# A Strassen-style up projection: one weight-block sum formed by an accumulating DMA instead of by VectorE

## The chip, the core and the metric

The kernel runs on one core of one Trainium2 chip. The metric is the device time of one launch in microseconds. Inside the core, TensorE (PE) multiplies matrices, VectorE (DVE) and ScalarE (ACT) work on elements, GpSimd (POOL) and SyncE (SP) here mostly issue transfers between the chip's main memory and the on-chip memory. Each engine runs its own list of instructions strictly in order. An instruction that waits for a semaphore holds up everything behind it on its engine. L124 means line 124 of the kernel before.

## The reference

A decoder trunk of two layers on 528 positions (512 tokens and 16 learned ones) of width 1024, in float32. The part that the change touches is the first matrix product of the MLP:

```
for l in range(DEPTH):
    a = rmsnorm(h, mix_pre_g[l])
    ...
    h = h + rmsnorm(y @ w_out[l], mix_post_g[l])
    a = rmsnorm(h, mlp_pre_g[l])
    f = jnp.square(jax.nn.relu(a @ w_up[l])) @ w_down[l]
    h = h + rmsnorm(f, mlp_post_g[l])
```

`w_up` is 1024 x 4096 and `w_down` 4096 x 1024 in each layer.

## The kernel before

**Matrix products.** Each float32 operand is split in a rounded part `hi` and the rest `lo`. A product is three matmuls, hi·hi, hi·lo and lo·hi (`mm3`, L193 to L195). A weight tile is loaded by SP into a raw buffer `wraw` (five buffers of 256 KB, taken in turn), then `cast` makes `hi` on ACT (L108) and `lo = raw - hi` on DVE (L109). Casts run ahead of PE: a tile is prepared as soon as PE has released an old one (`tile_done`, `refill`).

**The MLP.** It goes in four chunks of 1024 hidden columns per layer. A chunk is eight "up" tiles (`a @ w_up`, relu, square) and eight "down" tiles that add into `z`. In chunk 0 the up tiles are plain. In chunks 1 to 3 two up tiles at a time, a pair, are computed by Winograd's form of Strassen's method: seven products of half depth instead of eight. There are four pairs in a chunk, three such chunks in a layer, two layers, so six such chunks and 24 pairs. In what follows p0 to p3 are the four pairs of one chunk.

**Weights of a pair.** `prep_pair` prepares them in seven steps n = 0 to 6. At n = 0 SP loads four blocks A11, A21, A22, A12 of 512 x 128 (L119). Four sums are then formed on DVE, each one instruction on 128 x 512 elements: S1 = A21 + A22 (L124), S2 = A11 - S1 (L125), S3 = A21 - A11 (L128, in place of A21) and S4 = A12 + S2 (L131, in place of S2). The steps cast A11, S2, S3, S1, A12, A22, S4 in this order. S1 and S2 live in the pool `u`, which has two buffers, so the S1 of a pair has the buffer of the S1 of the pair before. That buffer is free once step n = 3 of the pair before has cast it.

**Products of a pair.** `fast_pair` does seven products of 12 matmuls each in four banks of the accumulation memory: into b1 with B11, into b6 with T2, into b7 with T3, into b5 with T1, then on top of what is there into b1 with B21, into b7 with T4, into b5 with B22. DVE empties the banks in between (L955): u2 = p1 + b6, u3 = u2 + b7, then u3 + b5. The product with T4 writes onto b7, so PE must wait until DVE has read b7 for u3. The product with B22 writes onto b5, so it must wait until DVE has read b5 for u3 + b5.

**The order of the work.** The program is written tile by tile. A scheduler then fixes each engine's order at build time, from its own estimate of when things will be ready. So an edit in `prep_pair` can move instructions everywhere in the lists, and DVE's list mixes casts and sums for the next two pairs with the emptying of banks for the pair that PE is working on.

Of the kernel before, what the change touches and what calls it, by code (L numbers as in the profile page):

```python
# [11 lines left out]
ALU = mybir.AluOpType  # L12

P = 128
# [22 lines left out]
def trunk_kernel(ctx, tc, xT, gains, sinkb, sinkm, rope, masks, maskm, ident_in, w_in, w_out, w_up, w_down, outT):  # L37
    nc = tc.nc
    ACT, DVE, POOL, PE = nc.scalar, nc.vector, nc.gpsimd, nc.tensor
# [64 lines left out]
    def half():  # L104
        return wp.tile([P, 4, P], F32, tag="wraw", name="wraw", bufs=5)

    def cast(raw, hi, lo):
        ACT.activation(hi, raw, AF.Copy)  # L108
        DVE.tensor_tensor(lo, raw, hi.bitcast(F32), ALU.subtract)  # L109


    pair = {}

    def prep_pair(l, m, n):

        if n == 0:
            for name, k, mm in (("A11", 0, m), ("A21", 0, m + 1), ("A22", 4, m + 1), ("A12", 4, m)):
                pair[name] = half()
                nc.sync.dma_start(pair[name], w_up[l].rearrange("(k p) m -> p k m", p=P)[:, k:k + 4, P * mm:P * mm + P])  # L119
        flat = lambda t: t.rearrange("p k m -> p (k m)")  # L120
        f = wp.tile([P, KT, P], F32R, tag="w", name="wf", bufs=2 * CAP)
        if n == 1:
            pair["S1"], pair["S2"] = (utile()[:, :512].rearrange("p (k m) -> p k m", k=4) for _ in range(2))
            DVE.tensor_tensor(pair["S1"], pair["A21"], pair["A22"], ALU.add)  # L124
            DVE.tensor_tensor(pair["S2"], pair["A11"], pair["S1"], ALU.subtract)  # L125
        if n == 2:
            pair["S3"] = pair["A21"]
            DVE.tensor_tensor(pair["S3"], pair["A21"], pair["A11"], ALU.subtract)  # L128
        if n == 6:
            pair["S4"] = pair["S2"]  # L130
            DVE.tensor_tensor(pair["S4"], pair["A12"], pair["S2"], ALU.add)  # L131
        cast(pair[("A11", "S2", "S3", "S1", "A12", "A22", "S4")[n]], f[:, 0:4, :], f[:, 4:8, :])
        prepared.append((f[:, 0:4, :], f[:, 4:8, :]))

    def prep(beside=None):
# [5 lines left out]
        if kind == "upx":  # L141
            return prep_pair(l, *sub)
# [105 lines left out]
    def utile():  # L248
        return tp.tile([P, L + 2], F32, tag="u", name="u", bufs=2)
# [855 lines left out]
```

## Time and profile before

| what | value |
|---|---|
| time before, median of 2 runs | 1141.0 us (1140.63 and 1141.37) |
| the profiled execution, device time | 1140.6 us |
| its span from first to last instruction | 1138.8 us |
| mean granted TensorE clock over the span | 0.975 |
| DMA, all queues, mean over the span | 102.04 MB, 90 GB/s |
| DMA queue of SP (q1) | 100.15 MB, 30.4% of 16 engines' time |
| DMA queue of POOL (q0) | 0.21 MB, 0.1% |

The profiled execution lies 1.8 us above its span, and 0.4 us below the median. Durations in the trace include pipeline fill: two instructions of one engine overlap in part, so the distance between starts is shorter than the duration of one.

### The profile page before, as it was taken

To read this page: it belongs to the slowest core of one execution; us is meant where nothing else is said; L and a number is where in the kernel's file an instruction comes from. 1 tells how busy PE (TensorE), PEld (TensorE's weight loads), DVE (VectorE), ACT (ScalarE), POOL (GpSimd) and SP (SyncE) were. 2 spreads that over 40 slices of the span, in tenths; PEclk is the share of its full clock that TensorE was granted. 3 is DMA by queue.
4 is the path that set the end of the run, shared out by engine and by line. 5 is a ranking of instruction groups with operands and counts; after the bars stand their busy time and mean duration, and the time that the engine had idled before them with its cause. 6 is when DMAs were issued, how large, how long until landed. Compare 5 with 4: busy or idle time off the path is not lost.

```text
span 1138.8 us, 21453 instructions
## 1 busy us (share of the span) xinstructions
PE 1088.9 (96%) x8066; PEld 1042.9 (92%) x8066; DVE 822.3 (72%) x1941; ACT 641.2 (56%) x1542; POOL 20.2 (2%) x56
## 2 busy tenths in 40 slices
PE   8999889899999999999989997898999999999995
PEld 8999789899999999999978997898888988988995
DVE  7987867868486586586689878678855856856836
ACT  8665766655383274275456556666734734724732
POOL 3000000000000000000000000000000000000001
PEclk9999989899999999999989999898999999999998
DMA  9242122242243243144132421222422522522502
GB/s 263 66 124 65 38 75 68 81 117 70 66 131 102 61 126 112 50 119 130 43 88 59 116 63 47 66 75 75 123 81 65 148 85 65 156 77 67 147 1 75
DMA packets 197672, 102.04 MB, mean 90 GB/s; under 512 B 7424, under 2 KB 197520, under 8 KB 197568
## 3 DMA queue, kind: packets, MB, share of 16 engines
q1 hardware_dynamic: 196960, 100.15, 30.4%
q8 instruction: 63, 1.03, 0.4%
q14 instruction: 41, 0.34, 0.1%
q10 hardware_dynamic: 432, 0.32, 0.1%
q0 software_dynamic: 176, 0.21, 0.1%
HBM read 97.88 MB, written 2.10 MB: 88 GB/s over the span
## 4 chain that ended last, share of the span: by engine, by line
PE 87%; DVE 7%; ACT 3%; issue 1%; DMA 1%; SPq 0%; DVEq 0%; POOL 0%; ACTq 0%
PE ps L195 28%; PE ps L193 28%; PE ps L194 27%; PE ps L199 2%; DVE wlo L109 1%; PE ps L232 1%; ACT S L647 1%; DMA h<-in_xT 1%; DVE acc L277 1%; PE ps L693 1%; DVE p L281 1%; DVE a_lo L335 0%; DVE S L658 0%; DVE z L706 0%; DVE h L324 0%
## 5 line engine op out<-in xcount | busy, mean ns | idle before, releaser
L194 PE MATMUL ps<-f_lo,whi 128*128 128x256 f32 (+2 forms) x1072 | 326.1, 305 | 0.0
L195 PE MATMUL ps<-f_hi,wlo 128*128 128x256 f32 (+2 forms) x1072 | 325.4, 305 | 0.0
L193 PE MATMUL ps<-f_hi,whi 128*128 128x256 f32 (+2 forms) x1072 | 323.7, 306 | 0.0
L193 PE MATMUL ps<-a_hi,whi 128*128 128x256 f32 (+3 forms) x808 | 242.5, 302 | 7.2 <-ACT a_hi L330 6.2
L194 PE MATMUL ps<-a_lo,whi 128*128 128x256 f32 (+3 forms) x808 | 238.5, 295 | 4.6 <-DVE a_lo L335 4.1
L195 PE MATMUL ps<-a_hi,wlo 128*128 128x256 f32 (+3 forms) x808 | 237.1, 294 | 0.3 <-DVE wlo L109 0.3
L194 PEld LDWEIGHTS ps<-f_lo,whi 128*128 128x128 f32 x1072 | 201.7, 188 | 9.6
L195 PEld LDWEIGHTS ps<-f_hi,wlo 128*128 128x128 f32 x1072 | 201.9, 189 | 9.2
L193 PEld LDWEIGHTS ps<-f_hi,whi 128*128 128x128 f32 x1072 | 200.1, 188 | 9.3
L108 ACT ACTIVATE whi<-wraw 128x512 fp32r<-128x512 f32 x264 | 153.8, 623 | 94.2 <-PE ps L194 65.6
L109 DVE TENSOR_TENSOR wlo<-wraw,whi 128x512 fp32r<-128x512 f32 x264 | 173.1, 686 | 44.0 <-ACT whi L108 21.3
L193 PEld LDWEIGHTS ps<-a_hi,whi 128*128 128x128 f32 x808 | 157.7, 196 | 11.9 <-ACT a_hi L330 8.2
L194 PEld LDWEIGHTS ps<-a_lo,whi 128*128 128x128 f32 x808 | 158.2, 196 | 9.3 <-DVE a_lo L335 6.5
L195 PEld LDWEIGHTS ps<-a_hi,wlo 128*128 128x128 f32 x808 | 158.5, 196 | 1.8 <-DVE wlo L109 0.5
L505 DVE TENSOR_TENSOR z<-z,ps 128x272 f32<-128x272 f32 (+2 forms) x78 | 37.9, 486 | 100.3 <-PE ps L195 100.2
L194 PE MATMUL ps<-a_lo,wf 128*128 128x264 f32 (+1 forms) x384 | 108.0, 283 | 0.0
L193 PE MATMUL ps<-a_hi,wf 128*128 128x264 f32 (+1 forms) x384 | 107.8, 283 | 0.0
L108 ACT ACTIVATE wf<-wraw 128x512 fp32r<-128x512 f32 x96 | 59.7, 626 | 84.3 <-PE ps L194 51.5
L195 PE MATMUL ps<-a_hi,wf 128*128 128x264 f32 (+1 forms) x384 | 107.1, 283 | 0.0
L108 ACT ACTIVATE wf<-u 128x512 fp32r<-128x512 f32 x72 | 45.2, 628 | 87.8 <-PE ps L194 73.6
L109 DVE TENSOR_TENSOR wf<-wraw,wf 128x512 fp32r<-128x512 f32 x96 | 65.5, 686 | 10.9 <-ACT wf L108 9.8
L194 PEld LDWEIGHTS ps<-a_lo,wf 128*128 128x128 f32 x384 | 72.2, 188 | 0.1
(179 smaller groups left out, 1833.9 us busy)
## 6 DMA issues: line engine op xcount, KB each, us to landing
wraw<-in_w_up SPq DMA_DIRECT2D x128, 256.0 KB
wraw<-in_w_down SPq DMA_DIRECT2D x128, 256.0 KB
wraw<-in_w_in SPq DMA_DIRECT2D x72, 256.0 KB
wraw<-in_w_out SPq DMA_DIRECT2D x32, 128.0 KB
wraw<-in_w_out SPq DMA_DIRECT2D x16, 256.0 KB
outT<-h SPq DMA_DIRECT2D x14, 128.0 KB
h<-in_xT SPq DMA_DIRECT2D x4, 272.0 KB
h<-in_xT SPq DMA_DIRECT2D x4, 256.0 KB
```

The costliest lines, as they stand in the source:

```text
L108: ACT.activation(hi, raw, AF.Copy)
L109: DVE.tensor_tensor(lo, raw, hi.bitcast(F32), ALU.subtract)
L193: PE.matmul(ps, whi, ahi, start=first, stop=False, skip_group_check=onto)
L194: PE.matmul(ps, whi, alo, start=False, stop=False, skip_group_check=onto)
L195: PE.matmul(ps, wlo, ahi, start=False, stop=last, skip_group_check=onto)
L199: PE.matmul(ps, a[n], b[n], start=first and n == 0, stop=last and n == 1)
L232: PE.matmul(ps, ones[:, which, :], acc, start=True, stop=more is None)
L277: return (eng or DVE).tensor_tensor(acc, acc, sq, ALU.add)
L281: DVE.tensor_tensor(lo, src, hi.bitcast(F32), ALU.subtract)
L505: DVE.tensor_tensor(zz, zz, ps, ALU.add)
L647: ACT.activation(S[:, i, keys], S[:, i, keys], AF.Exp, bias=ng[:, i:i + 1], accum_out=dn[:, i:i + 1])
L693: PE.transpose(bk[:, j * P:(j + 1) * P], S[:, j, kb * P:(kb + 1) * P], ident)
```

## The change

Two things are added and one is taken out. The sum S1 on DVE (L124) is gone. In its place SP loads A21 a second time, straight into the buffer of S1, and then POOL issues a DMA that reads A22 from main memory and adds it to that buffer (`accum_op=ALU.add`). So A21 and A22 are each read twice from main memory, once as blocks for the other sums and casts, once for S1. The buffers of S1 and S2 are taken at step n = 0 instead of n = 1. The space for the descriptors of POOL's DMAs grows from 1024 to 4096. Nothing else in the source differs; lines below L118 move by two (L125 becomes L127, L955 becomes L957).

```diff
         if n == 0:
+            src = lambda k, mm: w_up[l].rearrange("(k p) m -> p k m", p=P)[:, k:k + 4, P * mm:P * mm + P]
+            pair["S1"], pair["S2"] = (utile()[:, :512].rearrange("p (k m) -> p k m", k=4) for _ in range(2))
+            nc.sync.dma_start(pair["S1"], src(0, m + 1))
+            POOL.dma_start(pair["S1"], src(4, m + 1), accum_op=ALU.add)
             for name, k, mm in (("A11", 0, m), ("A21", 0, m + 1), ("A22", 4, m + 1), ("A12", 4, m)):
                 pair[name] = half()
-                nc.sync.dma_start(pair[name], w_up[l].rearrange("(k p) m -> p k m", p=P)[:, k:k + 4, P * mm:P * mm + P])
+                nc.sync.dma_start(pair[name], src(k, mm))
...
         if n == 1:
-            pair["S1"], pair["S2"] = (utile()[:, :512].rearrange("p (k m) -> p k m", k=4) for _ in range(2))
-            DVE.tensor_tensor(pair["S1"], pair["A21"], pair["A22"], ALU.add)
             DVE.tensor_tensor(pair["S2"], pair["A11"], pair["S1"], ALU.subtract)
...
-    nc = _bacc.Bacc("TRN2", target_bir_lowering=False, num_devices=1, dynamic_dma_scratch_size=1024)
+    nc = _bacc.Bacc("TRN2", target_bir_lowering=False, num_devices=1, dynamic_dma_scratch_size=4096)
```

How this moves the lists is shown at three places, all in chunk 3 of layer 0, the one that PE begins at 480.91 us in the trace.

The first place is SP's list around the blocks of p2 and p3. In the kernel before the names are A11, A21, A22, A12 of p2 (6368 to 6374) and of p3 (6520 to 6526):

```order
L119 DMA wraw_6368<-in_w_up 128x4x128
L119 DMA wraw_6370<-in_w_up 128x4x128
L119 DMA wraw_6372<-in_w_up 128x4x128
L119 DMA wraw_6374<-in_w_up 128x4x128
L119 DMA wraw_6520<-in_w_up 128x4x128
L119 DMA wraw_6522<-in_w_up 128x4x128
L119 DMA wraw_6524<-in_w_up 128x4x128
L119 DMA wraw_6526<-in_w_up 128x4x128
```

In the changed kernel u_6378 and u_6531 are the S1 buffers of p2 and p3:

```order
L123 DMA wraw_6382<-in_w_up 128x4x128
L123 DMA wraw_6384<-in_w_up 128x4x128
L123 DMA wraw_6386<-in_w_up 128x4x128
L119 DMA u_6378<-in_w_up 128x4x128
L123 DMA wraw_6388<-in_w_up 128x4x128
L123 DMA wraw_6535<-in_w_up 128x4x128
L123 DMA wraw_6537<-in_w_up 128x4x128
L123 DMA wraw_6539<-in_w_up 128x4x128
L119 DMA u_6531<-in_w_up 128x4x128
L123 DMA wraw_6541<-in_w_up 128x4x128
```

The load into S1 stands behind three of the pair's own blocks and ahead of its A12. It is not hoisted a pair ahead, since its buffer is free only when the S1 of the pair before has been cast. POOL's list has the 12 accumulating DMAs of a layer in a row, with nothing of that layer's MLP between them.

The second place is DVE's list where S2 of p2 stands, just as PE begins p0. Before (u_6394 is S1, u_6395 is S2 of p2; ps_6352 to ps_6355 are the banks b1, b6, b7, b5 of p0):

```order
L125 TENSOR_TENSOR u_6395<-wraw_6368,u_6394 128x512
L109 TENSOR_TENSOR wf_6376<-wraw_6368,wf_6376 128x512
L955 TENSOR_TENSOR t_6400<-t_6379,ps_6353 128x264
L109 TENSOR_TENSOR wf_6393<-u_6395,wf_6393 128x512
L955 TENSOR_TENSOR t_6418<-t_6400,ps_6354 128x264
L131 TENSOR_TENSOR u_6395<-wraw_6374,u_6395 128x512
L109 TENSOR_TENSOR wf_6414<-wraw_6370,wf_6414 128x512
L955 TENSOR_TENSOR t_6435<-t_6418,ps_6355 128x264
L109 TENSOR_TENSOR wf_6432<-u_6394,wf_6432 128x512
```

After (u_6378 is S1, u_6379 is S2 of p2; ps_6362 to ps_6365 are b1, b6, b7, b5 of p0):

```order
L127 TENSOR_TENSOR u_6379<-wraw_6382,u_6378 128x512
L109 TENSOR_TENSOR wf_6390<-wraw_6382,wf_6390 128x512
L957 TENSOR_TENSOR t_6411<-t_6393,ps_6363 128x264
L109 TENSOR_TENSOR wf_6407<-u_6379,wf_6407 128x512
L957 TENSOR_TENSOR t_6429<-t_6411,ps_6364 128x264
L133 TENSOR_TENSOR u_6379<-wraw_6388,u_6379 128x512
L109 TENSOR_TENSOR wf_6425<-wraw_6384,wf_6425 128x512
L130 TENSOR_TENSOR wraw_6537<-wraw_6537,wraw_6535 128x512
L957 TENSOR_TENSOR t_6446<-t_6429,ps_6365 128x264
L109 TENSOR_TENSOR wf_6443<-u_6378,wf_6443 128x512
```

S2 keeps its place: the three readings of b6, b7 and b5 of p0 still stand behind it. S3 of p3 (L130) has come in ahead of the reading of b5. The last row is the cast that frees the S1 buffer of p2.

The third place is DVE's list one pair later, where S2 of p3 stands. Before (u_6547 is S2 of p3; ps_6505 and ps_6506 are b6 and b7 of p1):

```order
L109 TENSOR_TENSOR wf_6528<-wraw_6520,wf_6528 128x512
L281 TENSOR_TENSOR f_lo_73<-t_6476,f_hi_72 128x264
L125 TENSOR_TENSOR u_6547<-wraw_6520,u_6546 128x512
L955 TENSOR_TENSOR t_6552<-t_6531,ps_6505 128x264
L281 TENSOR_TENSOR f_lo_73<-t_6498,f_hi_72 128x264
L955 TENSOR_TENSOR t_6570<-t_6552,ps_6506 128x264
L109 TENSOR_TENSOR wf_6545<-u_6547,wf_6545 128x512
```

After (u_6531 is S1, u_6532 is S2 of p3; ps_6516 to ps_6518 are b6, b7, b5 of p1):

```order
L109 TENSOR_TENSOR wf_6543<-wraw_6535,wf_6543 128x512
L127 TENSOR_TENSOR u_6532<-wraw_6535,u_6531 128x512
L957 TENSOR_TENSOR t_6564<-t_6546,ps_6516 128x264
L283 TENSOR_TENSOR f_lo_73<-t_6509,f_hi_72 128x264
L957 TENSOR_TENSOR t_6582<-t_6564,ps_6517 128x264
L109 TENSOR_TENSOR wf_6560<-u_6532,wf_6560 128x512
L109 TENSOR_TENSOR wf_6578<-wraw_6537,wf_6578 128x512
L133 TENSOR_TENSOR u_6532<-wraw_6541,u_6532 128x512
L957 TENSOR_TENSOR t_6599<-t_6582,ps_6518 128x264
```

Here too S2 stands ahead of the readings of b6, b7 and b5 of the pair that PE works on.

## The prediction

> **What bounds the kernel now.** I read the page first, then the stages of the trace, then the stage that the change touches.
>
> ```profile
> PE 1088.9 (96%) x8066; PEld 1042.9 (92%) x8066; DVE 822.3 (72%) x1941; ACT 641.2 (56%) x1542; POOL 20.2 (2%) x56
> ...
> PE 87%; DVE 7%; ACT 3%; issue 1%; DMA 1%; SPq 0%; DVEq 0%; POOL 0%; ACTq 0%
> ...
> L193 PE MATMUL ps<-a_hi,wf 128*128 128x264 f32 (+1 forms) x384 | 107.8, 283 | 0.0
> ...
> L124 DVE TENSOR_TENSOR u<-wraw 128x512 f32<-128x512 f32 x24 | 16.6, 691 | 19.8 <-DMA wraw<-in_w_up 19.8
> ```
>
> PE is busy 96% of the span, and 87% of the chain that ended last is PE. In the pair stage it waits for nothing: the first matmul of most products (L193, 384 of them) has 0.0 us of idle time ahead of it. The last row is what is taken out: 24 sums of 691 ns, which waited 19.8 us in all for the load of A22. All of that lies beside PE. The stretch of one chunk, and the opening stretch in which POOL's only transfers run, look like this (columns: stretch, length, busy time of PE, weight load, DVE, ACT, POOL, clock, DMA share, GB/s):
>
> ```profile
> 9.70:17.00 7.30, 6.94 (x41) 6.62 (x42) 7.23 (x14) 6.45 (x17) 4.07 (x8) 0.77 1.15 321
> 480.90:522.70 41.80, 41.80 (x346) 41.80 (x345) 34.98 (x71) 32.04 (x73) 0.70 (x3) 1.00 0.45 131
> ```
>
> In the chunk PE is busy for all of 41.80 us at a granted clock of 1.00, DVE for 34.98 (84%). So a lighter DVE can't shorten this stage: it has nothing to give PE. The question is only whether the change makes PE wait.
>
> **What is removed and what is added.** Removed: one DVE instruction per pair; starts of neighbouring ones lie 0.61 us apart, so 0.61 us of DVE in a pair of 10.4 us, worth 0 us as PE has no idle time there to fill. Added per pair: one SP issue of 0.37 us (SP issues in the rows below), which moves A12 and the next pair's blocks back by 0.37 us on SP's queue, covered by SP's waits for free buffers (row below); one POOL issue, on a queue that does nothing else in these stages (0.70 us of POOL in 41.80 us, memsets for the next layer that have long to wait); and 2 x 256 KB of transfers. The stretch moves 131 GB/s at a share of 0.45, so 291 GB/s at full share; 512 KB per 10.4 us are 50 GB/s, or 0.17 more share, 0.26 if the accumulate moves its bytes twice. The engines stay under 0.75: bandwidth costs nothing.
>
> ```profile
> SPq L119 <- DVE wf L109: 179.7, 50, 5.9
> ```
>
> SP waited 179.7 us in 50 waits at L119 for a cast to free a buffer, 3.6 us each, which is the cover for its 0.37 us.
>
> What is left is latency. S2 is the next instruction that needs S1. Before, S1 was made by DVE from blocks that had come one step earlier. Now S1 is two transfers in series, which can't begin before the S1 of the pair before is cast, and DVE stands at S2 until the second has landed, with the bank readings that PE needs behind it.
>
> **The window.** Rows of DVE and PE in the chunk begun at 480.91 us:
>
> ```profile
> 475.81 0.69 DVE L109 TENSOR_TENSOR wf<-u,wf 128x512 fp32r<-128x512 f32 x1
> ...
> 483.03 0.69 DVE L125 TENSOR_TENSOR u<-wraw,u 128x512 f32<-128x512 f32 x1
> 483.64 0.68 DVE L109 TENSOR_TENSOR wf<-wraw,wf 128x512 fp32r<-128x512 f32 x1
> 484.25 0.42 DVE L955 TENSOR_TENSOR t<-t,ps 128x264 f32<-128x264 f32 x1
> ...
> 485.49 0.43 DVE L955 TENSOR_TENSOR t<-t,ps 128x264 f32<-128x264 f32 x1
> 485.83 0.69 DVE L131 TENSOR_TENSOR u<-wraw,u 128x512 f32<-128x512 f32 x1
> ...
> 480.91 0.29 PE L193 MATMUL ps<-a_hi,wf 128*128 128x264 f32 x1
> ...
> 488.32 0.28 PE L193 MATMUL ps<-tx,wf 128*128 128x264 f32 x1
> ...
> 489.78 0.28 PE L194 MATMUL ps<-a_lo,wf 128*128 128x264 f32 x1
> ...
> 522.52 0.29 PE L193 MATMUL ps<-f_hi,whi 128*128 128x272 f32 x1
> ```
>
> The first row casts the S1 of p1 and frees its buffer at 476.50. S2 of p2 starts at 483.03 before: a window of 6.53 us. PE begins p0 at 480.91, the product with T4 at 488.32, that with B22 at 489.78, and leaves the chunk at 522.52, so a pair takes 41.61/4 = 10.40 us.
>
> **Price of the load.** DVE frees a buffer at the end of the first row, SP issues into it, and DVE takes the data after a wait for that DMA:
>
> ```profile
> 486.44 0.68 DVE L109 TENSOR_TENSOR wf<-wraw,wf 128x512 fp32r<-128x512 f32 x1
> ...
> 487.15 0.37 SPq L119 DMA_DIRECT2D wraw<-in_w_up  x1
> ...
> 490.11 0.69 DVE L124 TENSOR_TENSOR u<-wraw 128x512 f32<-128x512 f32 x1 [0.36 <-DMA wraw<-in_w_up]
> ```
>
> From 487.12 to 490.11 are 3.0 us from free buffer to use, for 256 KB.
>
> **Price of the accumulate, L.** No row shows one. The nearest rows are POOL's own issues at the start (KB, then us from issue to landing):
>
> ```profile
> mk<-in_masks POOLq DMA_DIRECT2D x1, 128.0 KB, 5.1
> ident<-in_ident POOLq DMA_DIRECT2D x1, 64.0 KB, 5.2
> ...
> sm<-in_sinkm POOLq DMA_DIRECT2D x1, 1.0 KB, 5.0
> ```
>
> 1 KB takes 5.0 us and 128 KB 5.1, so nearly all of it is a fixed cost of this way of issuing. They ran at a DMA share of 1.15, where engines were full; the chunk has 0.45. Lower end for L: 3.0 us, if without that crowd POOL's path were as quick as SP's. Upper end: 5.1 plus a whole further load of 3.0, so 8.1, since the accumulate reads and rewrites 256 KB. I take 5.5, nearest to the POOL rows: 5.1, plus 0.9 for 256 KB at 291 GB/s, less 0.5 for the emptier engines.
>
> [...]
>
> **What it does to PE.** Starts of DVE are 0.61 us apart for 512 columns (483.03, 483.64) and 0.35 for 264 (485.49, 485.83). Three more rows give the trip through ACT: S2 starts, its cast by ACT follows 0.78 later and ends 0.64 after that, and DVE's half of the cast starts 1.63 after S2.
>
> ```profile
> 494.84 0.69 DVE L125 TENSOR_TENSOR u<-wraw,u 128x512 f32<-128x512 f32 x1
> ...
> 495.62 0.64 ACT L108 ACTIVATE wf<-u 128x512 fp32r<-128x512 f32 x1 [0.38 <-DVE u L125]
> ...
> 496.47 0.69 DVE L109 TENSOR_TENSOR wf<-u,wf 128x512 fp32r<-128x512 f32 x1
> ```
>
> - S2 of p2 starts at 476.50 + 3.0 + L = 479.5 + L, at 5.5 so 485.0 instead of 483.03. Behind it, in the changed list, u3 starts 2.24 later and ends by 482.2 + L, in time for T4 at 488.32. S3 of p3 needs A21 of p3, whose buffer is that of A11 of p2, free 0.61 + 0.69 after S2 starts and loaded 3.05 later; so S3 starts at S2 + 4.35, u3 + b5 at S2 + 4.96, and the cast that frees S1 of p2 ends at S2 + 6.0, which is 485.5 + L.
> - S2 of p3 then starts at 485.5 + L + 3.0 + L = 488.5 + 2L, at 5.5 so 499.5 instead of 494.84. Behind it, in the changed list, come readings of b6, b7 and, after two casts and S4, b5, which ends 3.9 after S2: 492.4 + 2L. PE needs b5 of p1 at 489.78 + 10.40 = 500.2. PE waits 2L - 7.8 in this chunk in all; at 5.5 that is 3.2 us.
> - S2 of p1 falls in the down tiles before. Its window, by the next two rows, is 453.71 to 465.33, or 11.6 us, against 8.5. S2 of p0 has a whole down phase. Neither waits.
>
> ```profile
> 453.03 0.68 DVE L109 TENSOR_TENSOR wf<-u,wf 128x512 fp32r<-128x512 f32 x1
> ...
> 465.33 0.68 DVE L125 TENSOR_TENSOR u<-wraw,u 128x512 f32<-128x512 f32 x1
> ```
>
> The other chunks by the same steps from their rows:
>
> ```profile
> 300.49 0.69 DVE L109 TENSOR_TENSOR wf<-u,wf 128x512 fp32r<-128x512 f32 x1 [3.82 <-ACT wf L108]
> ...
> 305.59 0.29 PE L193 MATMUL ps<-a_hi,wf 128*128 128x264 f32 x1
> ...
> 950.74 0.68 DVE L109 TENSOR_TENSOR wf<-u,wf 128x512 fp32r<-128x512 f32 x1
> ...
> 955.53 0.28 PE L193 MATMUL ps<-a_hi,wf 128*128 128x256 f32 x1
> ```
>
> The distance from cast to PE's start is alike (4.4 and 4.1 us), but in the first chunk and in layer 1 the changed list has a bank reading ahead of S2 of p3 and frees S1 earlier: 2L - 9.0 for the first, 2L - 9.25 for each of the three of layer 1. Chunk 2 of layer 0 is as chunk 3. The sum is (2L - 9.0) + 2(2L - 7.8) + 3(2L - 9.25) = 12L - 52.4. At L = 5.5 that is 13.6 us. Casts of tiles lose some 5 us of a lead that is 16 us (S2's cast of 496.47 serves a product that PE reaches past 512), so weights don't run out. The profiled execution is 1140.6 us and gives 1154.2; it lies 0.4 under the median of 1141.0, and I write 1154.
>
> **Rivals.**
> 1. Hidden. If L is below about 4.5, every term is 0 or nearly so, and the time is 1141. For it: the window of 6.53 us less 3.0 leaves 3.5, the banks give 2 to 3 us more, and the POOL rows come from full engines. Against it: 5.0 us for 1 KB. [...]
> 2. Slower by over 2%. The accumulate itself is slow: 512 pieces of 512 bytes, each read twice and written back. The point from which it decides is 12L - 52.4 = 22.8, L = 6.3. At L = 7 the time is 1141 + 31.6 = 1173, at 8.1 it is 1141 + 44.8 = 1186. For it: nothing in the rows has these pieces, and each 1 us of L is paid twice a chunk. Against it: from 1 KB to 128 KB the rows grow by only 0.1 us.
> 3. Faster, since DVE has 24 x 0.61 = 14.6 us less to do and no more waits of 19.8 us at L124. At most 34 us, 1107, if DVE were on the path here. The 0.0 us of idle time in the pair stage speaks against it.
>
> **How the numbers follow.** Forecast (L from 4.5 to 6.3): 0.42, hidden 0.22, slow accumulate 0.33, faster 0.03. A measurement of this kernel can tell about 2% (22.8 us) from no change. Faster by over 2%: 0.03; within 2%: 0.42 + 0.22 = 0.64; slower: 0.33. The range goes from 1140, hidden, to 1186, the upper end for L; past it lie the faster case and accumulates above 8.1. The likeliest case alone spans 1142 to 1164.
>
> **What would show it.** In the changed profile: S2 with idle time ahead of it put down to the DMA into u, mainly on p2 and p3 of each chunk, some 2 and 4 us each; POOL's DMA rows of u with 5.5 us to landing; PE idle at T4 or B22 of p1, put down to DVE's bank readings, some 14 us in all; no wait of PE for wf. PE idle 0 in the pair stage would show the first rival, landing times above 6.3 the second. I would be wrong in kind if PE waits at the start of a chunk or for weights.

## The result, and the profile after

The changed kernel takes 1154.86 us, the median of two runs (1152.77 to 1156.94), against 1141.0 us before. The ratio is 1.0115, with a 95% interval of 1.0079 to 1.015: slower by about 13 us, and within 2%. The profiled execution is the one of 1156.94 us, with a span of 1155.2 us. Lines of the changed kernel from L118 on lie two below those of before (S2 is L127, the bank readings are L957, the three matmuls of a product L195 to L197).

The page of the changed kernel: busy time of the engines, POOL's queue (packets, MB, share of 16 engines), the chain that ended last by engine and by line, the first matmul of most products, and POOL's transfers into `u` (KB each, us from issue to landing).

```profile
PE 1095.7 (95%) x8066; PEld 1048.4 (91%) x8066; DVE 806.2 (70%) x1917; ACT 638.5 (55%) x1542; POOL 51.1 (4%) x80
...
q0 software_dynamic: 12848, 6.50, 4.5%
...
PE 76%; DVE 8%; DMA 8%; ACT 4%; issue 3%; SPq 0%; DVEq 0%; POOL 0%; POOLq 0%; ACTq 0%
PE ps L195 24%; PE ps L196 24%; PE ps L197 24%; DMA u<-in_w_up 6%; PE ps L201 2%; PE ps L234 1%; DVE wlo L109 1%; DVE wf L109 1%; DMA wraw<-in_w_up 1%; DVE acc L279 1%; PE ps L695 1%; ACT S L649 1%; DVE t L957 1%; ACT wf L108 1%; DMA wraw<-in_w_in 0%
...
L195 PE MATMUL ps<-a_hi,wf 128*128 128x264 f32 (+1 forms) x384 | 108.7, 286 | 0.0
...
u<-in_w_up POOLq DMA_DIRECT2D x24, 256.0 KB, 4.7
```

DVE is busy 16 us less than before (822.3), as its 24 sums are gone, and the time is longer. On the chain PE has gone from 87% to 76%, and transfers into `u` now hold 6%. That 6% is 69 us and is not what was lost: the chain follows one way back from the end, and where a transfer and PE end at nearly the same moment it can take either. (A kernel below that loses no time has 82% for PE and 3% for transfers there.) What was lost stands in the waits of PE (engine, line, what it waited for: us in all, times, longest):

```profile
PE ps L234 <- DVE acc L279: 21.5, 10, 7.6
PE ps L195 <- DVE t L957: 9.5, 6, 2.7
```

The first row is an old one from another stage. The second is new: six waits, one in each chunk of pairs, for a bank reading on DVE. The group of L195 above with 0.0 us of idle time doesn't show them, since they stand at products with another left operand (`tx`). DVE's own waits say what held it:

```profile
DVE u L127 <- DMA u<-in_w_up: 29.6, 13, 3.8
DVE wraw L130 <- DMA wraw<-in_w_up: 26.0, 18, 4.1
```

The first row is S2 waiting for S1's accumulate, the second S3 waiting for A21, whose buffer now comes free later. The whole course in one chunk (the third of layer 0), from the timeline of the changed kernel (start, length, engine, line, operation):

```profile
494.95 0.69 DVE L109 TENSOR_TENSOR wf<-u,wf 128x512 fp32r<-128x512 f32 x1
...
495.67 0.37 SPq L119 DMA_DIRECT2D u<-in_w_up  x1
...
499.31 1.30 POOL L120 DMA_DIRECT2D u<-in_w_up  x1 [13.17 <-DVE t L957]
...
503.48 0.28 PE L197 MATMUL ps<-a_hi,wf 128*128 128x264 f32 x1
...
503.88 0.69 DVE L127 TENSOR_TENSOR u<-wraw,u 128x512 f32<-128x512 f32 x1 [3.00 <-DMA u<-in_w_up]
...
505.17 0.42 DVE L957 TENSOR_TENSOR t<-t,ps 128x264 f32<-128x264 f32 x1
...
505.65 0.39 PE L195 MATMUL ps<-tx,wf 128*128 128x264 f32 x1 [1.89 <-DVE t L957]
```

The cast that frees the S1 of p2 ends at 495.64. SP loads A21 into it, POOL's accumulate of A22 starts 3.67 us later, and S2 of p3 starts at 503.88, 8.24 us after the buffer came free, having waited 3.00 us. (The row of POOL names a reading on DVE, because that ended last by the profile; 11 of POOL's 24 such waits are put down to the load into `u`, which the accumulate has to follow.) The readings behind it are late by as much, and PE, which reaches T4 of p1 at 503.60, starts it at 505.65.

**The sum doesn't close with the waits alone.** From the first to the last matmul on weights of pairs, the six chunks take 41.0 to 41.5 us each before and 42.84, 43.66, 45.14, 41.72, 43.28 and 47.13 us after: 16.2 us more in all. At the six waits the steps between matmul starts, less the usual 0.12 us, are 1.25, 2.09, 2.05, 0.59, 1.67 and 2.85, or 10.5 us. The rest is in the granted clock. Windows of the same chunk (length, busy time of PE, weight load, DVE, ACT, POOL, clock, DMA share, GB/s):

```profile
485.70:531.20 45.50, 43.61 (x346) 43.40 (x345) 34.38 (x70) 31.36 (x73) 2.44 (x5) 0.96 0.53 138
503.40:505.60 2.20, 0.36 (x3) 0.15 (x2) 1.72 (x5) 0.94 (x2) 0.00 (x0) 1.00 0.00 0
507.00:510.40 3.40, 3.40 (x18) 3.40 (x17) 3.36 (x8) 2.53 (x7) 0.19 (x1) 0.50 0.27 79
510.40:520.00 9.60, 9.60 (x81) 9.60 (x80) 7.43 (x16) 7.90 (x19) 0.00 (x0) 1.00 0.55 162
```

Shortly after the lull (second row) the clock is 0.50 for 3.4 us (third row): 18 matmuls there, where the fourth row has 29 in as much time. PE is "busy" all the while, so no view of waits shows this loss. The last chunk has 6.83 us of it. Together 10.24 us at half the clock cost 5.1 us, and 10.5 + 5.1 = 15.6 of the 16.2 us. Before, the granted clock in these chunks is 1.00 throughout.

### The profile page after: what moved, and what is told of

Its sections match the earlier page's. It is cut to its first block, busy times and chain, and to the rows that moved or that the text cites. A ratio compares the mean times of both kernels' runs of the same rounds, so it can differ in the third digit from the quotient of the medians.

```text
span 1155.2 us, 21561 instructions
## 1 busy us (share of the span) xinstructions
PE 1095.7 (95%) x8066; PEld 1048.4 (91%) x8066; DVE 806.2 (70%) x1917; ACT 638.5 (55%) x1542; POOL 51.1 (4%) x80
## 4 chain that ended last, share of the span: by engine, by line
PE 76%; DVE 8%; DMA 8%; ACT 4%; issue 3%; SPq 0%; DVEq 0%; POOL 0%; POOLq 0%; ACTq 0%
PE ps L195 24%; PE ps L196 24%; PE ps L197 24%; DMA u<-in_w_up 6%; PE ps L201 2%; PE ps L234 1%; DVE wlo L109 1%; DVE wf L109 1%; DMA wraw<-in_w_up 1%; DVE acc L279 1%; PE ps L695 1%; ACT S L649 1%; DVE t L957 1%; ACT wf L108 1%; DMA wraw<-in_w_in 0%
## 5 line engine op out<-in xcount | busy, mean ns | idle before, releaser
L196 PE MATMUL ps<-f_lo,whi 128*128 128x256 f32 (+2 forms) x1072 | 325.8, 305 | 0.0
L197 PE MATMUL ps<-f_hi,wlo 128*128 128x256 f32 (+2 forms) x1072 | 324.9, 305 | 0.0
L195 PE MATMUL ps<-f_hi,whi 128*128 128x256 f32 (+2 forms) x1072 | 324.0, 306 | 0.0
L195 PE MATMUL ps<-a_hi,whi 128*128 128x256 f32 (+3 forms) x808 | 242.4, 302 | 7.7 <-ACT a_hi L332 6.1
L196 PE MATMUL ps<-a_lo,whi 128*128 128x256 f32 (+3 forms) x808 | 238.6, 296 | 4.6 <-DVE a_lo L337 4.2
L197 PE MATMUL ps<-a_hi,wlo 128*128 128x256 f32 (+3 forms) x808 | 236.8, 293 | 0.0
L196 PEld LDWEIGHTS ps<-f_lo,whi 128*128 128x128 f32 x1072 | 201.5, 188 | 9.6
L197 PEld LDWEIGHTS ps<-f_hi,wlo 128*128 128x128 f32 x1072 | 201.8, 189 | 9.2
L195 PEld LDWEIGHTS ps<-f_hi,whi 128*128 128x128 f32 x1072 | 200.1, 188 | 9.3
L195 PEld LDWEIGHTS ps<-a_hi,whi 128*128 128x128 f32 x808 | 158.1, 196 | 12.1 <-ACT a_hi L332 8.0
L196 PEld LDWEIGHTS ps<-a_lo,whi 128*128 128x128 f32 x808 | 158.3, 196 | 9.5 <-DVE a_lo L337 6.5
L197 PEld LDWEIGHTS ps<-a_hi,wlo 128*128 128x128 f32 x808 | 158.5, 196 | 1.6 <-DVE wlo L109 0.3
L196 PE MATMUL ps<-a_lo,wf 128*128 128x264 f32 (+1 forms) x384 | 109.3, 286 | 0.0
L195 PE MATMUL ps<-a_hi,wf 128*128 128x264 f32 (+1 forms) x384 | 108.7, 286 | 0.0
L197 PE MATMUL ps<-a_hi,wf 128*128 128x264 f32 (+1 forms) x384 | 108.6, 286 | 0.0
L196 PEld LDWEIGHTS ps<-a_lo,wf 128*128 128x128 f32 x384 | 73.6, 192 | 0.2
```

The source lines that it names most:

```text
L195: PE.matmul(ps, whi, ahi, start=first, stop=False, skip_group_check=onto)
L196: PE.matmul(ps, whi, alo, start=False, stop=False, skip_group_check=onto)
L197: PE.matmul(ps, wlo, ahi, start=False, stop=last, skip_group_check=onto)
```

## The experiments

The theory: load and accumulate in turn take longer than the time between "S1 of p1 is cast" and "S2 of p2 is wanted", and the delay is passed on from p2 to p3, so that it counts twice in a chunk. I call C the time from the end of the cast that frees the buffer to the start of S2; in the changed kernel it is 8.35 us, the mean over p2 and p3. The prediction's sum of PE's waits, 12L - 52.4 with C = 3.0 + L, reads 12C - 88.4. The rivals: the traffic, the queues and the order that DVE is given. Each ratio below is against executions of the kernel before that were timed beside that experiment, so it doesn't follow from 1141.0.

**1. The changed kernel again**, with three kernels beside it.

> The changed kernel once more, beside the others on the same chip. Series theory: PE idle ahead of the first matmul with T4 of p1, once a chunk, 9 to 12 us in all, put down to DVE L957; time 1152 to 1157. What the profiled run lost beyond that (16.3 us against 10.5 us of such gaps) is put down to the granted clock, so a run at a clock of 0.975 should lie near 1152.

1156.26 us, ratio 1.013 (1.0109 to 1.0151). The waits at T4 are there again, 10.7 us in six by the view that gave 9.5 above; C is 8.43.

**2. A third buffer for S1 and S2.**

```diff
-        return tp.tile([P, L + 2], F32, tag="u", name="u", bufs=2)
+        return tp.tile([P, L + 2], F32, tag="u", name="u", bufs=3)
```

> The pool of S1 and S2 has three buffers instead of two, all else as changed. The load into S1 then waits for the cast of the last block of two pairs before (n = 6) instead of the cast of the S1 of the pair before, which is four casts or some 5.8 us earlier. Series theory (load and accumulate in series behind the S1 of the pair before, DVE held at S2, PE held at T4 of p1): the chain of 8.3 us then ends before DVE comes to S2, DVE waits under 1 us in all for the DMA into u at p2 and p3, PE waits 0 at T4, time 1141 to 1143. Traffic theory (12.6 MB more, and POOL writing descriptors, slow other loads or engines): nothing changes, 1153 to 1156. Order theory (the scheduler's new lists cost it): about as changed, 1150 or more.

1142.27 us, ratio 1.0004 (0.9994 to 1.0014). The same 24 loads and 24 accumulates are issued, each landing 4.9 us after its issue in the median, and no wait for L957 is left among PE's waits. S2 of p2 no longer waits. S2 of p3 still waits for the accumulate, 2.1 us in the mean, where under 1 us in all was expected, but PE doesn't feel it. The chain of work that ended last is back where it was:

```profile
PE 87%; DVE 7%; ACT 3%; DMA 1%; issue 1%; DVEq 0%; SPq 0%; POOL 0%; ACTq 0%
```

So the two transfers cost nothing when they needn't wait for that buffer. But the scheduler also placed S2 of p3 anew here, ahead of the last two readings of p0, so this kernel alone doesn't tell the wait from the order. Experiment 6, whose lists are those of the changed kernel, does.

**3. The order alone.** The source as changed, but S1 by DVE in every pair (`m < 0` never holds).

```diff
-            nc.sync.dma_start(pair["S1"], src(0, m + 1))
-            POOL.dma_start(pair["S1"], src(4, m + 1), accum_op=ALU.add)
+            if m < 0:
+                nc.sync.dma_start(pair["S1"], src(0, m + 1))
+                POOL.dma_start(pair["S1"], src(4, m + 1), accum_op=ALU.add)
...
         if n == 1:
+            if not (m < 0):
+                DVE.tensor_tensor(pair["S1"], pair["A21"], pair["A22"], ALU.add)
```

> Written as the changed kernel, buffers of S1 and S2 taken at n = 0 and the larger space for descriptors, but S1 is formed by DVE in all 24 pairs; no second load, no accumulate. Series theory: 1141, within 2 us. Traffic theory: 1141. Order theory, if taking the buffers earlier is what counts: 1150 or more.

1140.77 us, ratio 0.9994 (0.9985 to 1.0004). Taking the buffers a step earlier and the larger space for descriptors cost nothing.

**4. The traffic alone.** S1 by DVE; both transfers go into a third buffer that nobody reads.

```diff
-            pair["S1"], pair["S2"] = (utile()[:, :512].rearrange("p (k m) -> p k m", k=4) for _ in range(2))
-            nc.sync.dma_start(pair["S1"], src(0, m + 1))
-            POOL.dma_start(pair["S1"], src(4, m + 1), accum_op=ALU.add)
+            pair["S1"], pair["S2"], extra = (utile()[:, :512].rearrange("p (k m) -> p k m", k=4) for _ in range(3))
+            nc.sync.dma_start(extra, src(0, m + 1))
+            POOL.dma_start(extra, src(4, m + 1), accum_op=ALU.add)
...
+            DVE.tensor_tensor(pair["S1"], pair["A21"], pair["A22"], ALU.add)
...
-        return tp.tile([P, L + 2], F32, tag="u", name="u", bufs=2)
+        return tp.tile([P, L + 2], F32, tag="u", name="u", bufs=3)
```

> S1 is formed by DVE as before. The second load of A21 and the accumulate of A22 run as in the change, on SP and POOL, but into a third buffer that nothing reads. All transfers of the change, none of its waits on DVE. Series theory: PE waits 0 at T4, 1141 to 1143. Traffic theory: 1150 or more, with longer waits for loads of w_up.

1140.99 us, ratio 0.9994 (0.9985 to 1.0004). Bandwidth and the queues of SP and POOL cost nothing that can be measured.

**5. The load without the accumulate.**

```diff
             nc.sync.dma_start(pair["S1"], src(0, m + 1))
-            POOL.dma_start(pair["S1"], src(4, m + 1), accum_op=ALU.add)
```

> Leaves out the accumulating transfer, so S1 is A21 alone. Series theory (load and accumulate in turn, 8.3 us from free buffer to S2, are longer than the window of 6.5 us and are paid twice a chunk): the load alone is 3.6 us, fits the window, and S2 of p2 and p3 comes as early as before; no wait of PE at T4 of p1, time 1141 us (1140 to 1143). Rival, the load into u is what hurts (SP's queue now begins a pair with a transfer that waits for a buffer of u, and A11 to A12 stand behind it): most of the loss stays, 1150 to 1156 us.

1140.3 us, ratio 0.9995 (0.9986 to 1.0005). The load into `u` by itself fits the window.

**6. A plain copy in place of the accumulate.**

```diff
-            POOL.dma_start(pair["S1"], src(4, m + 1), accum_op=ALU.add)
+            POOL.dma_start(pair["S1"], src(4, m + 1))
```

> The second transfer is issued by GpSimd as before, 256 KB of A22 into the same buffer, but as a plain copy; the addition is left out. Fixed-cost theory (what the accumulate costs is GpSimd's way of issuing, 1.3 us of issue and some 3 us more, and the order behind the load): landing 4.2 to 4.8 us after the issue starts, S2 of p2 and p3 8 us or a little more after the free buffer, PE waits at T4 of p1 in all six chunks, 1149 to 1157 us. Rival, the reading and rewriting of the buffer is the cost: landing 3.6 us or less, S2 at 7 us, time 1141 to 1144 us.

1140.89 us, ratio 0.9996 (0.9987 to 1.0006): the rival's time, not that of my theory of a fixed cost. Every engine's list is that of the changed kernel; only the kind of transfer differs. Its rows for the tile `u`, the landing time and PE's wait at T4, one fence for each view (ns of POOL's issue as min/median/max; us to landing; us, times, longest):

```profile
L120 POOL DMA_DIRECT2D u<-in_w_up x24: 749/749/776, 148.9 to 1052.1; - x24
```

```profile
q0 software_dynamic: 2096, 6.50, 2.1%
...
u<-in_w_up POOLq DMA_DIRECT2D x24, 256.0 KB, 3.4
```

```profile
PE ps L195 <- DVE t L957: 0.8, 2, 0.4
```

The copy lands 1.3 us earlier than the accumulate (3.4 against 4.7), and C is 7.38. There 12C - 88.4 is 0.2 us, but four of its six terms have gone below 0, which a wait can't; the other two leave 1.9 us. The waits are gone but for 0.8 us. So the changed order costs nothing by itself, and a transfer from POOL as such does fit, by a hair; what tips the balance is what accumulating adds to it. Two things are left: its issue is longer (0.75 against the row below), with 80 packets a transfer against 528 (q0's packets less the 176 of before, over 24), and its bytes are added. The changed kernel:

```profile
L120 POOL DMA_DIRECT2D u<-in_w_up x24: 1273/1292/1362, 150.1 to 1065.1; - x24
```

**7. and 8. Fewer and more pieces.** The accumulate of 256 KB adds other data of the same matrix, in 128 pieces of 2 KB, or in 1024 of 256 bytes.

```diff
-            POOL.dma_start(pair["S1"], src(4, m + 1), accum_op=ALU.add)
+            POOL.dma_start(pair["S1"].rearrange("p k m -> p (k m)"), w_up[l][P * (m % 8):P * (m % 8) + P, 512:1024], accum_op=ALU.add)
```

```diff
-            POOL.dma_start(pair["S1"], src(4, m + 1), accum_op=ALU.add)
+            POOL.dma_start(pair["S1"].rearrange("p k (h m) -> p (k h) m", h=2), w_up[l].rearrange("(k p) m -> p k m", p=P)[:, :, P * m + P:P * m + P + 64], accum_op=ALU.add)
```

> The accumulate adds other data of w_up: 256 KB from 128 pieces of 2 KB in place of 512 pieces of 512 bytes, so S1 is not A21 plus A22. GpSimd's plain copy of A22 landed 3.4 us after its issue began and cost nothing, the accumulate 4.7 us. Theory of the pieces (the accumulate is slower because it goes piece by piece, 528 packets a transfer against 80): with 128 pieces the issue is below 0.9 us, the landing 3.3 to 3.9 us, S2 7.0 to 7.5 us after the free buffer, time 1140 to 1143 us. Rival, the adding itself (256 KB read and written back): issue may shrink, the landing stays above 4.2 us, S2 at 8 us, time 1147 to 1157 us.

> The accumulate adds other data of w_up in 1024 pieces of 256 bytes, so S1 is not A21 plus A22; the order of the work differs somewhat from the changed kernel, so the transfer's own rows count more than the time. Theory of the pieces: twice the 512 pieces, so the issue grows from 1.3 to about 2.4 us and the landing by 1.3 us or more, to 6.0 to 7.5 us; S2 comes 10 us or more after the free buffer and the time is 1170 to 1195 us. Rival, the bytes: landing 4.5 to 5.0 us as now, 1150 to 1160 us.

With 128 pieces 1150.15 us, ratio 1.0068 (1.0042 to 1.0095); with 1024 pieces 1156.98 us in one run, landing 5.2 us after the issue began (median). The first has the changed kernel's lists but for two places in layer 1; in the second they differ in more. Two views of the kernel with 128 pieces, the tile's row and the page:

```profile
L120 POOL DMA_DIRECT2D u<-in_w_up x24: 866/872/933, 149.6 to 1058.8; - x24
```

```profile
q0 software_dynamic: 3632, 6.50, 3.7%
...
u<-in_w_up POOLq DMA_DIRECT2D x24, 256.0 KB, 4.4
```

And the issue of the one with 1024 pieces:

```profile
L120 POOL DMA_DIRECT2D u<-in_w_up x24: 1550/1567/1640, 150.2 to 1066.9; - x24
```

Take the issue from the landing time and the parts come apart:

| 256 KB from POOL | issue, us | issue to landing, us | landing less issue, us |
|---|---|---|---|
| plain copy | 0.75 | 3.4 | 2.65 |
| accumulate, 128 pieces | 0.87 | 4.4 | 3.5 |
| accumulate, 512 pieces (the change) | 1.29 | 4.7 | 3.4 |
| accumulate, 1024 pieces | 1.57 | 5.2 | 3.6 |

Pieces cost time in the issue, 0.7 us from 128 to 1024; adding costs some 0.8 to 1.0 us after it, with no clear trend in the pieces. Of the 1.3 us that the accumulate is slower than a copy, 0.5 are issue and 0.8 the adding. Neither theory had it whole: the rival of 128 pieces (landing above 4.2, 1147 to 1157 us) came true, that of 1024 pieces (4.5 to 5.0, 1150 to 1160 us) nearly, and the theory of the pieces has only the smaller part.

**9. The accumulate twice**, one after the other.

```diff
             POOL.dma_start(pair["S1"], src(4, m + 1), accum_op=ALU.add)
+            POOL.dma_start(pair["S1"], src(4, m + 1), accum_op=ALU.add)
```

> A22 is accumulated twice, one transfer after the other, so S1 is A21 plus twice A22. Series theory: the chain from free buffer to S2 grows from 8.3 to 8.3 + 4.8 = 13.1 us, and each us of it is paid twice in each of six chunks. The changed kernel's waits of 10.5 us at 8.3 give 12 C - 89, so 68 us at 13.1, 1209 us; the window of p1 (11.6 us) is passed too, by 1.5 us, so up to 9 us more, and longer waits of PE bring more stretches at half the granted clock, up to 3 us for each of six or twelve: 1209 to 1245 us. Rival, paid once a chunk (only the first delay counts and p3 catches up): 6 x 4.8 = 29 us more than the changed kernel, 1184 us. Rival, the second transfer overlaps the first: 1155 to 1165 us.

1197.42 us, ratio 1.0495 (1.0477 to 1.0512): below my range and above both rivals. C is 13.45, close to the 13.1 expected, so the transfers do run one after the other. But PE doesn't wait where the sum has it (lines here lie one further down: L196 is the first matmul of a product, L958 the bank reading):

```profile
PE ps L196 <- DVE t L958: 22.2, 10, 5.6
...
PE ps L196 <- ACT t L968: 14.3, 6, 3.7
```

There are 16 waits, not 6, and none stands at T4 of p1. The long ones are at T4 of p0 or the product behind it, and at the product with B21 of p2, which must wait until ACT has copied p1 out of b1 (L968). The scheduler orders the lists by its own estimates of durations, and with two accumulates it put one or two readings of p0 ahead of S2 of p2 and three of p1 ahead of S2 of p3, where the changed kernel has none and at most one. So this was not the same list with a longer wait, and the 12C of the changed list doesn't hold for it: it gives 73 us, and these waits are 36.5. Half the clock comes back here at each of the longer lulls, seven of which are 3 us or more. The first of them:

```profile
335.80:340.20 4.40, 0.66 (x6) 0.45 (x5) 4.40 (x10) 4.40 (x13) 0.00 (x0) 1.00 0.56 162
340.20:343.60 3.40, 3.40 (x18) 3.40 (x17) 3.40 (x8) 3.01 (x8) 1.29 (x1) 0.50 0.69 201
343.60:347.00 3.40, 3.40 (x30) 3.40 (x29) 3.09 (x7) 2.49 (x7) 0.00 (x0) 1.00 1.17 239
```

The six chunks are 60.1 us longer than before. 30.7 us of them ran at half the clock, worth 15.4 us, which leaves 44.7 us for longer steps.

**10. to 12. One place at a time.** The sum by transfers in some pairs only, by DVE in the others: first in p0 and p1 (as shown), then in p2 (`m % 8 == 4`), then in p3 (`m % 8 == 6`).

```diff
-            nc.sync.dma_start(pair["S1"], src(0, m + 1))
-            POOL.dma_start(pair["S1"], src(4, m + 1), accum_op=ALU.add)
+            if m % 8 in (0, 2):
+                nc.sync.dma_start(pair["S1"], src(0, m + 1))
+                POOL.dma_start(pair["S1"], src(4, m + 1), accum_op=ALU.add)
...
+            if not (m % 8 in (0, 2)):
+                DVE.tensor_tensor(pair["S1"], pair["A21"], pair["A22"], ALU.add)
```

> The sum by transfers in pairs p0 and p1 of each chunk alone, in p2 and p3 by VectorE; the output is the reference's. Series theory: p0 has a whole down phase and p1 a window of 9.7 to 11.6 us, both longer than 8.3, so 1141 us (1140 to 1143) with 12 of the 24 sums moved. Rival, each moved sum costs its share wherever it stands (queues, traffic, order): half of the loss, 1147 to 1149 us.

1141.3 us, ratio 0.9999 (0.9989 to 1.0009): half of the sums moved, at no cost.

> The sum by transfers in p2 of each chunk alone. Series theory: S2 of p2 starts some 1.8 us later than before, and bank readings behind it still come before PE needs them; no second delay is added, so PE waits 0 to 0.5 us a chunk: 1141 to 1143 us. Rival, each delay costs by itself: half of the loss or more, 1147 to 1149 us.

1141.04 us, ratio 0.9996 (0.9984 to 1.0008). S2 of p2 comes 7.9 to 9.8 us after the free buffer, where the window was 6.2 to 7.4, and all six chunks are as long as before to 0.01 us: the delay of one pair is swallowed by the lead of the bank readings.

> The sum by transfers in p3 of each chunk alone. Series theory: with S1 of p2 on VectorE the S1 buffer comes free as early as before, S2 of p3 starts some 2 us later than before, less than the lead of the bank readings (2.0 to 3.0 us by the slack that the changed kernel's waits leave): PE waits 0 to 1 us a chunk, 1141 to 1146 us; the whole loss is more than the losses of p2 alone and p3 alone added. Rival, the loss of the changed kernel is all p3's own: 1153 to 1156 us.

1143.3 us, ratio 1.0013 (1.0003 to 1.0023): 1.5 us, some 0.3 to 2.6. The parts add to 0 + 0 + 1.5 us; together they cost 13 to 15. The loss is made by the delay of p2 being handed on to p3, and the traces show the handing on. Counted from the first matmul of the chunk, in the mean of six, the buffer for p3 comes free at 8.05 us with p3 alone and at 9.63 us in the changed kernel; S2 of p3 follows at 16.43 and at 17.99 us, with the same C (8.38 and 8.36). What p3 is later by, 1.56 us a chunk, is what p2 freed the buffer later by, 1.58 us.

## Why the prediction was right, and where its terms were off

1. *A lighter DVE gives PE nothing.* Right: 16 us less of DVE, and the kernel without the wait (three buffers, ratio 1.0004) is no faster than before.
2. *SP's and POOL's queues and the bandwidth cost nothing.* Right, by the kernel with the traffic alone (ratio 0.9994). The DMA share went from 0.44 to 0.47 in the six chunks to 0.50 to 0.65.
3. *The load, 3.0 us from free buffer.* Too low: on p2 and p3 POOL's issue starts 3.64 us after the free buffer in the mean, 3.4 to 4.4.
4. *The accumulate, L = 5.5 us from POOL's start to S2.* Too high: 4.71 in the mean on p2 and p3. The two errors cancel, 8.35 where the sum had 8.5, and that is luck. The reason given for 5.5 was also off. It read the rows of 5.0 to 5.2 us at the start as the fixed cost of POOL's way of issuing; in the chunk a plain copy of 256 KB lands in 3.4. The crowd for which I took off 0.5 us may explain the rest of the difference; no run here measured it. And I had no term for the adding, some 0.8 us, and the longer issue, 0.5.
5. *S2 of p2 and p3 wait some 2 and 4 us, S2 of p0 and p1 don't cost.* Right in place, and somewhat too high for p3: 2.07 us before S2 of p2 and 3.00 before S2 of p3 in the chunk shown, 1.6 and 3.2 in the mean of six; p0 and p1 alone cost nothing.
6. *S3 waits for a late A21, and weights don't run out.* Right, in the row of L130 above; and PE waits for no `wf`.
7. *PE waits at T4 or B22 of p1, 13.6 us in all.* The place is right: T4 of p1 in all six chunks. The size is 10.5 us of steps. With the measured C of 8.35 the sum gives 11.8. Part of the rest is a wrong reading in the terms of chunks 2 and 3 of layer 0. They count to the end of the reading of b5, which the product with B22 needs; but PE was held one product earlier, by the reading of b7, and behind T4 it went on without a wait. By the prediction's own steps that reading ends 1.73 us after S2 of p3, at 490.2 + 2L, and T4 of p1 wants it at 488.32 + 10.40 = 498.72, so the term is 2L - 8.5 and not 2L - 7.8. At L = 5.35 that is 2.2 us against 2.9; measured are 2.09 and 2.05. At C = 7.96 (128 pieces) the sum has 7.1, and the ratio gives a loss of 7.8 us (4.8 to 10.8), of which the clock has 1.7 in the profiled execution. The terms leave 0 at their own values of C: 7.25 us for these two with the term put right, 7.5 to 7.6 for the others. A plain copy with 7.38 stands at that edge, the accumulate one microsecond past it.
8. *No term at all* stood for the clock. It cost 5.1 us in the profiled execution of the changed kernel and 1.7 in that of its repetition. It filled up what the waits had less than forecast, so 1154 against 1154.86 is closer than the terms are. (Put on the median of 1141.0 instead of the profiled execution, the 13.6 us give 1154.6.)
9. *The rivals.* The hidden case needed L below about 4.5, so C below 7.5, and was missed by 0.9 us; the kernel with a plain copy is that case. The slow accumulate was not seen: on p2 and p3 it took 4.6 to 5.0 us, not above 6.3. The faster case never had a way.

The forecast called 2% what a measurement can tell. The loss of 1.15% was told apart from none, and the experiments separate 0.13%.

## What to carry to other kernels

Moving a sum from an engine into the transfers replaces work that can be done beside other work by latency in series: add up "free buffer to use" for the whole chain of transfers and compare it with the window in the trace (here 8.35 us against 6.2 to 7.4), and look whether one step's delay opens the next one's window later, since then it counts again. Where the window is short, try a further buffer: here it took the whole cost away (1142.27 against 1154.86 to 1156.26 us); but the sum was worth nothing in the first place, because the engine that it freed was not the one that bounds the stage. And where a busy TensorE is made to wait for a few microseconds, look at the granted clock behind the lull: here 10.5 us of waits were followed by 10.24 us at half the clock, which cost 5.1 us more (1.7 in the repetition).

## What the runs showed of the hardware

**After 13 of 19 lulls of over 2 us the granted clock was 0.5 for 3.4 us or twice that.** In five traces (the changed kernel and its repetition, the double accumulate, 128 and 1024 pieces) PE's matmul starts lie over 1.1 us apart at 34 places in the pair stage (steps from start to start, the usual 0.12 us among them). After all ten steps of 2.83 us or more the granted clock fell to 0.5, for 3.41 or 6.83 us; after nine steps of 2.04 to 2.60 us it did so three times (2.08, 2.17 and 2.57); after the 15 shorter ones never. In the changed kernel it fell after steps of 2.17 us (for 3.41 us) and 2.97 us (for 6.83 us), and stayed at 1.00 after those of 1.37, 1.79 and 2.21 us: between 2.04 and 2.60 us the length alone doesn't tell. The drop began before PE had started again or up to 1.5 us behind: in the changed kernel 1.30 us behind the start after the step of 2.17 us, and 0.77 us before the one that ended the step of 2.97 us. Windows of the last chunk of the changed kernel show the double length:

```profile
1067.00:1070.20 3.20, 1.23 (x11) 1.02 (x9) 0.36 (x1) 0.00 (x0) 0.00 (x0) 0.99 0.68 82
1070.20:1077.00 6.80, 6.08 (x28) 6.08 (x29) 6.37 (x15) 5.37 (x12) 0.00 (x0) 0.50 0.38 113
1077.00:1083.00 6.00, 6.00 (x53) 6.00 (x52) 4.65 (x11) 4.40 (x11) 0.00 (x0) 1.00 0.39 113
```

**An accumulating transfer of 256 KB was dearer than a copy in two places**, as the table above has it: its issue on POOL grew with the number of pieces (0.87 us for 128, 1.29 for 512, 1.57 for 1024, against 0.75 for a plain copy of the same 512 pieces), and some 0.8 to 1.0 us came on top before it landed. The packets of POOL's queue show it too: 80 for a copy, 144 for an accumulate of 128 pieces, 528 for one of 512.
